# Second layer of a two-block transformer kernel: two projection chunks and eight convolution taps moved to other places in the order

## The chip, the cores and the metric

The kernel runs on one core of a Trainium2 chip. Its engines work side by side, each through its own list of instructions in the written order: TensorE (PE, matmuls; PEld is its weight load), VectorE (DVE), ScalarE (ACT), GpSimd (POOL), and SyncE (SP), which issues the DMAs. The metric is the device time of one execution in microseconds (us). Before the change the median of 3 runs is 1493.54 us (1491.67 to 1496.65).

## The reference, cut to what matters

Two blocks follow each other: a two-layer block over 256 latents `x` and 256 context rows `ctx`, and a second one over the latents alone. The change lies in the mixers of the first block's second (last) layer, where the context gives only keys and values:

```
h  = rmsnorm(x,  g_pre_mix) * (1 + sc1)  + sh1
hc = rmsnorm(xc, g_pre_mix) * (1 + sc1c) + sh1c
u  = h @ w_in
if last:
    uc_mla_kv = hc @ w_in[:, MLA_Q_END:MLA_KV_END]
    uc_na_kv  = hc @ w_in[:, NA_Q_END:]
...
kv = heads(rmsnorm(ckv, g_kv) @ w_ukv)          # the latents' norm, over 128 columns
q  = heads(rmsnorm(cq, g_q) @ w_uq)
y_mla = softmax attention over latents and context
y_cf  = silu(layernorm(dwconv(a * sigmoid(g), w_dw) + b_dw)) @ w_pw      # 31 taps
nq, nk, nv = split(u[..., CF_END:], 3)
y_na  = neighbourhood attention of nq over nk, nv and the context's nk, nv
y = concatenate([y_sc, y_mla, y_cf, y_na]) @ w_out
```

## The kernel before, in words

**Products.** Every big product is exact to about fp32: an operand is split into a high part `H` (ACT copies it, rounded) and a low part `L` (the rest, subtracted on DVE or POOL), and `mm3` (L428) issues three matmuls, H by H, L by H and H by L. `step` (L336) splits one unit of weights, 128 by 1024, so: one ACT row at L373, one DVE or POOL row at L375. Units come in the order of `weight_plan`; `pump(n)` splits them until unit n is split, `unit(name, lead)` takes the next one after having `lead` more split behind it (default 4). There are 6 buffers for split units.

**The stage.** `block1_mixers` of the second layer works on activations transposed, channels on partitions and tokens along the row: columns 0 to 255 the latents, 256 to 511 the context. A `flat_chunk` is one unit by all tokens, 24 matmuls into one PSUM bank; 256 columns wide for a chunk of the latents alone (`cq`, `nq`, `sc_*`), 512 for `nk`, which the context needs too. There are 8 banks. The order before is:

1. `token_block`: the latents' keys and values by token (`tok` of tiles 0 and 1), then `latent_chunks` (`cq0`, `cq1`), then `ctx_part`: the context's normed rows are transposed on PE (`hT`), scaled (`hF`) and split into `hH` and `hL` on ACT and DVE, eight of each; then `latent_scales` (`cqss`, and a small rsqrt chain on ACT and DVE); then `pump` splits `nq0` and `nq1`; then `tok` of tiles 2 and 3, the context.
2. The rows of `tok` are copied out, their squares summed, and `normed` makes `ckvn`, the normed latents, from them: a short chain ACT, DVE, ACT.
3. `nq0`; `kv_transposed` (PE turns `ckvn` and `kr4`, ACT copies out `ckvT`); `nq1`; `latent_heads` (`kn`, `q`, `vm`).
4. `attention`: 11 slots. Slot i computes the scores `S` of item i (0 to 3 MLA, 4 to 7 neighbourhood), turns the probabilities of item i-2 (`PT`) and multiplies those of item i-3 by the values (`PV`). Each softmax is a chain: DVE takes the maximum, ACT the exponential, DVE the reciprocal, DVE and ACT the scaling. Between them stand fillers, put into the slots by their costs: `nk0`, `nk1`, six chunks of a short convolution (`sc_*`), and the first products of `w_out` (`o`). The conformer branch ends among the slots in a layer norm (`lnT`, `lnB`) and the pointwise product `pw`, put at slots 5, 7 and 9 (`CF_SLOTS`).

**Taps.** The conformer's convolution has 31 taps for each of two channel halves: half 0 on DVE (L1019), half 1 as an ACT row (L1025) and a POOL row (L1026). They stand in two queues, and `background(n0, n1)` issues the next n0 and n1 of them wherever it is called: after `tok` (2 for each tile, half 0 alone), in each `flat_chunk` (4 and 4 in this layer unless told otherwise) and in each slot (1 and 1). What is left when `lnT` comes is issued there.

The scheduler is off (`manual_schedule`), so each engine's order is the order of the Python calls.

Of the kernel before, what the change touches and what calls it, by code (L numbers as in the profile page):

```python
# [42 lines left out]
MODS = 8, 2, 2, 2, 2, 2, 2  # L43
# [14 lines left out]
TOK_TAPS = 3, 2  # L58
# [18 lines left out]
def _r(a, n):  # L77
    return np.arange(a, a + n)
# [17 lines left out]
def weight_plan():  # L96

    p = []

    def u(name, fn):  # L100
        p.append(("u", name, fn))

    left = []

    def mods(n):
        for _ in range(n):
            if left:
                l, v, k = left.pop(0)
                p.append(("u", ("mod", l, v, k), lambda w, l=l, v=v, k=k:
                          w["w_mod"][l][128 * k:128 * k + 128, 1024 * v:1024 * v + 1024]))  # L110

    def chunk(key, l, c0, name):
        u(name, lambda w, l=l, c0=c0: _stationary(w[key][l], _r(c0, 128)))

    left += [(0, v, q) for v in (0, 2, 4, 3, 5) for q in range(8)]
    left += [(1, v, q) for v in (1, 0, 2, 4, 3, 5) for q in range(8)]
    for l in range(2):
        n_in = 1 if l == 0 else 0
        if l == 0:
            for k in range(0, 8, 4):  # L120
                for nm, c0 in (("a", 1184), ("g", 1440)):
                    u(f"{nm}_{k}", lambda w, c0=c0, k=k: _stationary(w["w_in"][0][128 * k:128 * k + 512], _r(c0, 256)))
            mods(8)
        else:
            for m in range(2):
                chunk("w_in", l, 1184 + 128 * m, f"a{m}")
                chunk("w_in", l, 1440 + 128 * m, f"g{m}")
        for j in range(4):
            u(f"tok{j}", lambda w, l=l, j=j: _moving(w["w_in"][l], (2 * j, 2 * j + 1), TOK_COLS))
        mods(MODS[0] * n_in)  # L130
        for nm, c0 in (("cq", 768), ("nq", 1696), ("nk", 1952)):
            for m in range(2):
                chunk("w_in", l, c0 + 128 * m, f"{nm}{m}")
                mods(n_in * MODS[{"cq": 1, "nq": 3, "nk": 5}[nm] + m])
        for m in range(2):
            for j, (i, nm) in enumerate(((2, "sc_c"), (0, "sc_x"), (1, "sc_b"))):
                chunk("w_in", l, 256 * i + 128 * m, f"{nm}{m}")
                mods(n_in * SC_MODS[3 * m + j])
        for h in range(2):
            for j, kk in enumerate(OUT_ORDER):  # L140
                u(f"out{h}", lambda w, l=l, kk=kk, h=h: _moving(w["w_out"][l], kk, _r(512 * h, 512)))
                mods(n_in * OUT_MODS[4 * h + j])
        if l == 0:
            for g in range(9):
                if g < 8:
                    for j in range(4):
                        chunk("w_mlp1", l, 512 * g + 128 * j, "m1")
                        mods(M1_MODS[g][j])
                if g > 0:
                    for j in range(4):  # L150
                        u("m2", lambda w, l=l, c=4 * (g - 1) + j: _moving(w["w_mlp2"][l], (c,), _r(0, 1024)))
                    mods(sum(M2_MODS[g]))
            mods(100)
        else:
            def down(c):
                u("m2", lambda w, l=l, c=c: _moving(w["w_mlp2"][l], (c,), _r(0, 1024)))

            for b in range(2):
                for j in range(4):
                    u(f"m1_{b}", lambda w, l=l, j=j, b=b: _moving(w["w_mlp1"][l], (2 * j, 2 * j + 1), _r(512 * b, 512)))  # L160
            for j, ds in zip(range(8, 32), MLP_DOWN):
                chunk("w_mlp1", l, 128 * j, "m1")
                for c in ds:
                    down(c)
            for c in range(26, 32):
                down(c)
    for nm in B2_BLOCKS:
        for j in range(4):
            u(nm, lambda w, j=j, c=B2_COL[nm]: _moving(w["w_in_2"][0], (2 * j, 2 * j + 1), _r(c, 512)))
    for m in range(16):  # L170
        chunk("w_in_2", 0, 6144 + 128 * m, "gate")
    for mm in range(4):
        for key in ("w_a_out_2", "w_b_out_2"):
            u(key, lambda w, key=key, mm=mm: np.concatenate(
                [_stationary(w[key][0], _r(256 * mm + 128 * i, 128)) for i in range(2)], 1))
    for h in range(2):
        for j in range(4):
            u(f"mix{h}", lambda w, j=j, h=h: _moving(w["w_mix_out_2"][0], (2 * j, 2 * j + 1), _r(512 * h, 512)))
    for b in range(2):
        for j in range(4):  # L180
            u(f"up_{b}", lambda w, j=j, b=b: _moving(w["w_up_2"][0], (2 * j, 2 * j + 1), _r(2816 * b, 512)))

    def down2(c):
        u("down", lambda w: _moving(w["w_down_2"][0], (c,), _r(0, 1024)))

    for j, ds in zip(range(4, 22), FFN_DOWN):
        chunk("w_up_2", 0, 128 * j, "up_g")
        chunk("w_up_2", 0, 2816 + 128 * j, "up_v")
        for c in ds:
            down2(c)  # L190
    for c in range(16, 22):
        down2(c)
    return p
# [110 lines left out]
class Program:  # L304
# [952 lines left out]
            y[k] = (self.k2("yH", dt=F32R), self.k2("yL", dt=F32R))  # L1257
        return y[k]

    def token_block(self, l, h, T):  # L1260

        nc, v = self.nc, self.nc.vector
        self.pool_l = False
# [7 lines left out]
        for ts in TOK_SETS[l]:  # L1271
            if ts[0] == CTX_AT and self.ctx_part:
                if self.narrow:
                    self.latent_chunks(l, h, T)
                self.ctx_part()
                self.ctx_part = None
                if self.narrow:
                    self.latent_scales(l, T)
                    self.pump(self.used + 1)
            banks = [self.ps("tok") for _ in ts]  # L1280
            for j in range(4):
                for i in range(2):
# [7 lines left out]
            for t in ts:  # L1290
# [5 lines left out]
                ps = banks.pop(0)  # L1296
# [5 lines left out]
                ps = None  # L1302
# [6 lines left out]
                                    m[:, :, None, 32:].to_broadcast([128, 2, 4, 32]), op=ALU.add)  # L1309
                elif t == 3:  # L1310
                    v.tensor_copy(kr[:, 2:4], u2[:, :, None, 128:160].to_broadcast([128, 2, 4, 32]))
            self.background(TOK_TAPS[l] * len(ts))

        def normed():
            r = self.rsqrt(ss, 4)
# [5 lines left out]
        us = a = b = u = u2 = None  # L1321
        if self.narrow:
            normed()
        else:
            self.latent_chunks(l, h, T, normed)

# [316 lines left out]
    def block1_mixers(self, l, h):  # L1643


        nc, v = self.nc, self.nc.vector
        full = l == 0
        T = 512 if full else 256
        nt = T // 128
        ranges = [(0, T)]  # L1650
        y = {}
        self.narrow = not full
        self.conformer_in(l, h, ranges, T)
        self.mla_w = ([self.k2("wuq") for _ in range(2)], self.k2("wukv"), [self.k2("cst") for _ in range(2)])
        s = self.ap["small"][l]
        for m in range(2):
            nc.sync.dma_start(self.mla_w[0][m], s[:, 512 * m:512 * m + 512])
        nc.sync.dma_start(self.mla_w[1], s[:, 1024:1536])
        for m in range(2):
            nc.sync.dma_start(self.mla_w[2][m], self.ap["c1"][:, 512 * m:512 * m + 512])  # L1660
        self.token_block(l, h, T)
        self.NQ, self.NK = [], []

        def nqk(dst, nm, n):
            ps = self.flat_chunk(nm, h, [(0, n)])
            q = self.k2(nm)
            nc.scalar.activation(q[:, :n], ps[:, :n], AF.Copy, scale=0.125 if dst is self.NQ else 1.0)
            dst.append(q)

        sc = self.short_conv(l, 0, h, ranges, T, y) + self.short_conv(l, 1, h, ranges, T, y)  # L1670
        nqk(self.NQ, "nq0", T)
        if full:
            self.latent_scales(l, T)
        self.kv_transposed(l)
        nqk(self.NQ, "nq1", T)
        self.latent_heads(l, T)
        self.mla_w = None
        sets = 2 if full else 1
        m = 4 * sets
        cost = 2.56 * sets  # L1680
        fl = [(lambda m=m: nqk(self.NK, f"nk{m}", 512), 5.1, 0, "") for m in range(2)]
        fl += [(f, cost, 0, "sc") for f in sc]
        banks = []

        def first(j):
            return [(f, 2.56, (0, CF_SLOTS[l][2] + 1, m + AHEAD + 1, 0)[j], "sc", 1) for f in self.out_parts("out", OUT_ORDER, y, nt, j, banks)]

        def gates():
            self.ga = self.gate_rows(l, 0, nt // 2)

        cf = self.conformer_out(l, T, y)
        fl += first(0) + first(1) + [(gates, 0.0, 0, "")]
        if full:
            fl += first(2)
        self.attention(l, sets, y, fl, dict(zip(CF_SLOTS[l], cf)))
        self.NQ = self.NK = self.VN = None
        if full:
            for f in first(3):
                f[0]()
        self.y, self.banks = y, banks  # L1700
# [823 lines left out]
```

## Time and profile before

| | |
|---|---|
| median of 3 runs | 1493.54 us |
| the profiled execution, its own time | 1495.41 us |
| its span | 1493.2 us |
| PE busy | 1428.6 us (96%) |
| PEld busy | 1194.3 us (80%) |
| DVE busy | 941.1 us (63%) |
| ACT busy | 768.4 us (51%) |
| POOL busy | 544.0 us (36%) |
| shares of the chain that ended last | PE 72%, DVE 16%, ACT 8%, issue 2%, DMA 1% |

Busy time is a share of the whole span; a busy PE is not PE at its peak, since matmuls overlap and their ends are modelled, so that a matmul's cost in a row of equal ones is the distance between two starts. The stage of the change lies between 664 and 816 us. In a row of the timeline the first number is the start in us from the span's start, the second the duration; in brackets stands how long the engine was idle ahead of it and what released it.

### The profile page before, as it was taken

The numbers are of one execution on the slowest core, as the hardware profiler recorded it, in microseconds if no ns is written. First come the engines' busy times: TensorE is split into PE (matmuls) and PEld (weight loads), VectorE is DVE, ScalarE is ACT, GpSimd is POOL, SyncE is SP. The second block draws the span as 40 slices with busy tenths as digits, with TensorE's granted clock in tenths as the row PEclk, the third lists the DMA queues.
The fourth block names the chain that finished last, engine by engine and source line by source line (L and its number), as shares of the span: only waits on it lengthen the run. The fifth ranks groups of instructions, "written<-read, shape, count | busy, mean of one in ns | idle before, by whom it ended". The sixth has DMA issues, their size and how long they took to land.

```text
span 1493.2 us, 21581 instructions
## 1 busy us (share of the span) xinstructions
PE 1428.6 (96%) x8260; PEld 1194.3 (80%) x8260; DVE 941.1 (63%) x1642; ACT 768.4 (51%) x1406; POOL 544.0 (36%) x351
## 2 busy tenths in 40 slices
PE   8989999999999998998899899998999999999998
PEld 7766767888778787877777689996888899789997
DVE  4685573765866676788776765556466666754335
ACT  4446564555553323345666554455434664556554
POOL 2384531203551500007263500005022555738882
PEclk9999999999999999998999999999999999999999
DMA  9653631124554553634242455555555433545551
GB/s 342 211 199 142 140 110 69 60 83 165 178 194 160 191 204 130 220 146 149 87 84 93 142 187 180 187 180 189 180 188 190 138 122 113 203 148 186 177 190 57
DMA packets 73103, 235.71 MB, mean 158 GB/s; under 512 B 13536, under 2 KB 14248, under 8 KB 73000
## 3 DMA queue, kind: packets, MB, share of 16 engines
q1 hardware_dynamic: 72280, 233.65, 46.3%
q8 instruction: 65, 1.06, 0.3%
q10 hardware_dynamic: 720, 0.69, 0.1%
q14 instruction: 38, 0.31, 0.1%
HBM read 233.27 MB, written 1.05 MB: 157 GB/s over the span
## 4 chain that ended last, share of the span: by engine, by line
PE 72%; DVE 16%; ACT 8%; issue 2%; DMA 1%; SPq 0%; DVEq 0%; ACTq 0%
PE m L431 8%; PE m L432 8%; PE m L430 8%; PE acc L430 3%; PE acc L431 3%; PE acc L432 3%; DVE L L375 3%; PE pj L431 2%; PE pj L430 2%; PE pj L432 2%; PE up L430 2%; PE up L432 2%; PE up L431 2%; ACT H L373 2%; ACT P L1447 1%
## 5 line engine op out<-in xcount | busy, mean ns | idle before, releaser
L375 POOL TENSOR_TENSOR L<-raw,H 128x1024 fp32r<-128x1024 f32 x117 | 283.3, 2443 | 323.0 <-ACT H L373 305.6
L373 ACT ACTIVATE H<-raw 128x1024 fp32r<-128x1024 f32 x314 | 317.3, 1050 | 131.4 <-PE m L432 48.1
L375 DVE TENSOR_TENSOR L<-raw,H 128x1024 fp32r<-128x1024 f32 x197 | 254.6, 1321 | 90.4 <-ACT H L373 87.8
L367 POOL TENSOR_TENSOR uL<-raw,uH 128x512 fp32r<-128x512 f32 x32 | 46.1, 1472 | 192.1 <-ACT uH L366 192.1
L431 PE MATMUL m<-hL,H 128*128 128x512 f32 (+1 forms) x304 | 109.0, 358 | 2.0 <-DVE hL L875 2.0
L430 PE MATMUL m<-hH,H 128*128 128x512 f32 (+1 forms) x304 | 109.0, 358 | 1.0 <-ACT hH L874 1.0
L432 PE MATMUL m<-hH,L 128*128 128x512 f32 (+1 forms) x304 | 108.7, 358 | 1.2 <-DVE L L375 1.2
L431 PE MATMUL m<-L,hidH 128*128 128x512 f32 x256 | 101.7, 397 | 4.2 <-DVE L L375 4.2
L1807 ACT ACTIVATE rl<-m 128x512 f32<-128x512 f32 (+1 forms) x56 | 28.3, 505 | 150.3 <-PE m L432 150.1
L430 PE MATMUL m<-H,hidH 128*128 128x512 f32 x256 | 101.7, 397 | 3.9 <-DVE hidL L1815 3.9
L432 PE MATMUL m<-H,hidL 128*128 128x512 f32 x256 | 100.7, 393 | 0.0
L690 POOL TENSOR_TENSOR macc<-mt,macc 128x512 f32<-128x512 f32 x42 | 61.1, 1494 | 92.3 <-ACT mt L688 92.3
L1026 POOL TENSOR_TENSOR cfacc<-cft,cfacc 128x512 f32<-128x512 f32 (+1 forms) x60 | 64.6, 1077 | 54.7 <-ACT cft L1025 50.8
L430 PE MATMUL up<-h,H 128*128 128x256 f32 x288 | 81.8, 284 | 0.0
L432 PE MATMUL up<-h,L 128*128 128x256 f32 x288 | 81.5, 283 | 0.0
L431 PE MATMUL up<-h,H 128*128 128x256 f32 x288 | 81.5, 283 | 0.0
L1814 DVE TENSOR_TENSOR m<-m,rl 128x512 f32<-128x512 f32 (+1 forms) x56 | 32.7, 584 | 76.6 <-ACT rl L1807 76.4
L696 DVE SCALAR_TENSOR_TENSOR macc<-raw,csil,macc 128x512 f32<-128x512 f32 x98 | 66.9, 749 | 0.0
L431 PEld LDWEIGHTS m<-hL,H 128*128 128x128 f32 x304 | 57.7, 190 | 10.9 <-DVE hL L875 2.6
L432 PEld LDWEIGHTS m<-hH,L 128*128 128x128 f32 x304 | 57.8, 190 | 10.1 <-DVE L L375 2.0
L430 PEld LDWEIGHTS m<-hH,H 128*128 128x128 f32 x304 | 57.9, 190 | 9.2 <-ACT hH L874 1.2
L2099 POOL TENSOR_TENSOR ra<-ra,rb 128x512 f32<-128x512 f32 x16 | 21.6, 1351 | 113.8 <-DVE rb L2097 113.3
(547 smaller groups left out, 4060.5 us busy)
## 6 DMA issues: line engine op xcount, KB each, us to landing
raw<-in_wst SPq DMA_DIRECT2D x208, 1024.0 KB
mod<-in_wmod SPq DMA_DIRECT2D x16, 256.0 KB
X<-in_x SPq DMA_DIRECT2D x4, 512.0 KB
nab<-in_rpb SPq DMA_DIRECT2D x32, 64.0 KB
raw<-in_wst SPq DMA_DIRECT2D x2, 512.0 KB
wuq<-in_small SPq DMA_DIRECT2D x4, 256.0 KB
cst<-in_c SPq DMA_DIRECT2D x4, 256.0 KB
grow<-in_rows SPq DMA_DIRECT2D x4, 256.0 KB
```

Source lines behind the costliest of these rows:

```text
L367: nc.gpsimd.tensor_tensor(lo, src, hi, op=ALU.subtract)
L373: nc.scalar.activation(hi, t[:, j, :], AF.Copy)
L375: (nc.gpsimd if pool else nc.vector).tensor_tensor(lo, t[:, j, :], hi, op=ALU.subtract)
L430: mm(out, a[0], b[0], start=start, stop=False)
L431: mm(out, a[0], b[1], start=False, stop=False)
L432: mm(out, a[1], b[0], start=False, stop=stop)
L690: nc.gpsimd.tensor_tensor(o, t, o, op=ALU.add)
L696: v.scalar_tensor_tensor(acc[i][j], a, c, o, op0=ALU.mult, op1=ALU.add)
L1026: nc.gpsimd.tensor_tensor(acc, t, acc, op=ALU.add)
L1807: nc.scalar.activation(r[:, :T], ps[:, :T], AF.Relu)
L1814: v.tensor_tensor(ps[:, :T], ps[:, :T], r[:, :T], op=ALU.mult)
L2099: self.nc.gpsimd.tensor_tensor(a, a, b, op=ALU.add)
```

## The change

In the second layer alone (`self.narrow`): `nq0` is issued inside `token_block`, behind `latent_scales` and ahead of `tok` of the context, where `pump` stood, with one unit split ahead and no taps; `nk0` is issued where `nq0` stood, ahead of `kv_transposed`, with two units split ahead and no taps, and the attention's list of fillers begins with `nk1`; the four taps of half 0 behind `tok` of the context are issued after `normed` instead of ahead of it; and the weights' order in this layer has `nk0` ahead of `nq1`. The first layer keeps its order.

```
@@ weight_plan
-        for nm, c0 in (("cq", 768), ("nq", 1696), ("nk", 1952)):
-            for m in range(2):
-                chunk("w_in", l, c0 + 128 * m, f"{nm}{m}")
-                mods(n_in * MODS[{"cq": 1, "nq": 3, "nk": 5}[nm] + m])
+        for nm, m in (("cq", 0), ("cq", 1), ("nq", 0), *((("nq", 1), ("nk", 0)) if l == 0 else (("nk", 0), ("nq", 1))),
+                      ("nk", 1)):
+            chunk("w_in", l, {"cq": 768, "nq": 1696, "nk": 1952}[nm] + 128 * m, f"{nm}{m}")
+            mods(n_in * MODS[{"cq": 1, "nq": 3, "nk": 5}[nm] + m])
@@ token_block
-    def token_block(self, l, h, T):
+    def token_block(self, l, h, T, nq):
...
                 if self.narrow:
                     self.latent_scales(l, T)
-                    self.pump(self.used + 1)
+                    nq()
...
-            self.background(TOK_TAPS[l] * len(ts))
+            if not self.narrow or ts[-1] < 3:
+                self.background(TOK_TAPS[l] * len(ts))
...
         if self.narrow:
             normed()
+            self.background(2 * TOK_TAPS[l])
@@ block1_mixers
-        self.token_block(l, h, T)
         self.NQ, self.NK = [], []
 
-        def nqk(dst, nm, n):
-            ps = self.flat_chunk(nm, h, [(0, n)])
+        def nqk(dst, nm, n, lead=None, taps=None):
+            ps = self.flat_chunk(nm, h, [(0, n)], lead, taps)
...
+        self.token_block(l, h, T, lambda: nqk(self.NQ, "nq0", T, 1, (0, 0)))
         sc = self.short_conv(l, 0, h, ranges, T, y) + self.short_conv(l, 1, h, ranges, T, y)
-        nqk(self.NQ, "nq0", T)
         if full:
+            nqk(self.NQ, "nq0", T)
             self.latent_scales(l, T)
+        else:
+            nqk(self.NK, "nk0", 512, 2, (0, 0))
         self.kv_transposed(l)
...
-        fl = [(lambda m=m: nqk(self.NK, f"nk{m}", 512), 5.1, 0, "") for m in range(2)]
+        fl = [(lambda m=m: nqk(self.NK, f"nk{m}", 512), 5.1, 0, "") for m in range(len(self.NK), 2)]
```

In the program's rows a name ends in the numbers of its buffer; `H_1318` and `L_1318` are `nq0`'s weights, `H_1319` is the second of the pair. On PE, behind the context's transposes, before:

```order
L1365 MATMUL cqss_1311_6546<-ones_150,cqs_1297_6490 128x1
L430 MATMUL tok_1321_6577<-H_1233_6133,hH_1200_6031 128x448
L431 MATMUL tok_1321_6577<-L_1233_6134,hH_1200_6031 128x448
L432 MATMUL tok_1321_6577<-H_1233_6133,hL_1201_6032 128x448
```

And the same place in the changed program:

```order
L1368 MATMUL cqss_1311_6546<-ones_150,cqs_1297_6490 128x1
L430 MATMUL nq0_1321_6577<-hH_1200_6031,H_1318_6567 128x256
L431 MATMUL nq0_1321_6577<-hL_1201_6032,H_1318_6567 128x256
L432 MATMUL nq0_1321_6577<-hH_1200_6031,L_1318_6568 128x256
```

The 24 rows of `nq0` now stand between `cqss` and the 48 rows of `tok`; its first row reads `H_1318`, its third `L_1318`.

On ACT the end of the context's split, `latent_scales` and what follows, before:

```order
L868 ACTIVATE hF_1310_6540<-hT_1306_6519,modT_1_0_4825,modT_1_1_4442 128x256
L874 ACTIVATE hH_1212_6043<-hF_1309_6536 128x256
L874 ACTIVATE hH_1214_6045<-hF_1310_6540 128x256
L450 ACTIVATE rs_y2_1314_6554<-cqss_1312_6551,eps_151 128x2
L451 ACTIVATE rs_y2_1314_6554<-rs_y2_1314_6554 128x2
L373 ACTIVATE H_1318_6567<-raw_1226_6097 128x1024
L373 ACTIVATE H_1319_6571<-raw_1226_6097 128x1024
L1298 ACTIVATE VN_1323_6627<-tok_1321_6577 128x256
```

And in the changed program:

```order
L868 ACTIVATE hF_1310_6540<-hT_1306_6519,modT_1_0_4825,modT_1_1_4442 128x256
L874 ACTIVATE hH_1212_6043<-hF_1309_6536 128x256
L874 ACTIVATE hH_1214_6045<-hF_1310_6540 128x256
L450 ACTIVATE rs_y2_1314_6554<-cqss_1312_6551,eps_151 128x2
L451 ACTIVATE rs_y2_1314_6554<-rs_y2_1314_6554 128x2
L373 ACTIVATE H_1318_6567<-raw_1226_6097 128x1024
L373 ACTIVATE H_1319_6571<-raw_1226_6097 128x1024
L1669 ACTIVATE nq0_1322_6602<-nq0_1321_6577 128x256
L373 ACTIVATE H_1325_6654<-raw_1235_6141 128x1024
L1299 ACTIVATE VN_1326_6658<-tok_1323_6604 128x256
```

`H_1318` stands at the same place on ACT in both programs, behind the context's last `hH` and the two rows of `latent_scales`; behind it the changed program has `nq0`'s copy and one more split, `H_1325`, which is `nq1`'s.

On DVE the rows about the latents' norm (`rs_*4`, which leads to `ckvn`) and up to the first `QT`, before:

```order
L1311 COPY kr4_1287_6393<-kv_1324_6628 128x256
L1019 SCALAR_TENSOR_TENSOR cfacc_1289_6398<-cfz_1_0_6210,cfw1_651,cfacc_1289_6398 128x256 x4
L452 TENSOR_SCALAR rs_x4_1327_6642<-kvss_1266_6320,eps_151 128x4
L458 TENSOR_TENSOR rs_z4_1329_6644<-rs_y4_1328_6643 128x4
L459 TENSOR_TENSOR rs_z4_1329_6644<-rs_z4_1329_6644,rs_x4_1327_6642 128x4
L460 TENSOR_SCALAR rs_z4_1329_6644<-rs_z4_1329_6644 128x4
L463 TENSOR_TENSOR rs_y4_1328_6643<-rs_y4_1328_6643,rs_z4_1329_6644 128x4
L375 TENSOR_TENSOR L_1331_6658<-raw_1235_6141,H_1331_6657 128x1024
L375 TENSOR_TENSOR L_1332_6662<-raw_1235_6141,H_1332_6661 128x1024
L375 TENSOR_TENSOR L_1334_6668<-raw_1248_6247,H_1334_6667 128x1024
L1019 SCALAR_TENSOR_TENSOR cfacc_1289_6398<-cfz_1_0_6210,cfw1_651,cfacc_1289_6398 128x256 x4
L1340 COPY KTe_1344_6726<-krT_1342_6715 64x512
```

And in the changed program:

```order
L1312 COPY kr4_1287_6393<-kv_1327_6659 128x256
L452 TENSOR_SCALAR rs_x4_1330_6669<-kvss_1266_6320,eps_151 128x4
L458 TENSOR_TENSOR rs_z4_1332_6671<-rs_y4_1331_6670 128x4
L459 TENSOR_TENSOR rs_z4_1332_6671<-rs_z4_1332_6671,rs_x4_1330_6669 128x4
L460 TENSOR_SCALAR rs_z4_1332_6671<-rs_z4_1332_6671 128x4
L463 TENSOR_TENSOR rs_y4_1331_6670<-rs_y4_1331_6670,rs_z4_1332_6671 128x4
L1019 SCALAR_TENSOR_TENSOR cfacc_1289_6398<-cfz_1_0_6210,cfw1_651,cfacc_1289_6398 128x256 x4
L375 TENSOR_TENSOR L_1334_6689<-raw_1235_6141,H_1334_6688 128x1024
L1343 COPY KTe_1341_6733<-krT_1339_6722 64x512
```

Four taps moved behind the norm's chain, and the four that `nq0` issued before are gone from here; they stand in the attention's slot 2, where the changed program has five taps of half 0 and the one before one; slots 0, 1 and 3 have 5, 5 and 4 in both.

## Rows read from the trace of the kernel before

**Rows 1.** Timeline of PE, 710 to 728 us, cqss to nq0

```profile
710.33 1.10 PE L1365 MATMUL cqss<-ones,cqs 128*128 128x1 f32 x8
712.81 0.47 PE L430 MATMUL tok<-H,hH 128*128 128x448 f32 x1 [1.38 <-ACT hH L874]
...
720.05 0.37 PE L430 MATMUL tok<-H,hH 128*128 128x448 f32 x1
...
724.39 0.28 PE L430 MATMUL nq<-hH,H 128*128 128x256 f32 x1
...
727.14 0.28 PE L432 MATMUL nq<-hH,L 128*128 128x256 f32 x1
```

**Rows 2.** Timeline of ACT, then of DVE, 717 to 722 us

```profile
717.76 0.30 ACT L450 ACTIVATE rs_y<-cqss,eps 128x2 f32<-128x2 f32 x1 [0.59 <-DVE cqss L1368]
...
718.20 1.99 ACT L373 ACTIVATE H<-raw 128x1024 fp32r<-128x1024 f32 x2
...
719.28 2.36 DVE L375 TENSOR_TENSOR L<-raw,H 128x1024 fp32r<-128x1024 f32 x2
```

**Rows 3.** Windows: busy us of PE, PEld, DVE, ACT, POOL, granted clock, DMA

```profile
86.00:88.00 2.00, 0.27 (x2) 0.12 (x2) 1.98 (x3) 0.00 (x0) 2.00 (x2) 1.00 0.73 281
...
712.00:714.00 2.00, 1.19 (x5) 0.97 (x6) 1.52 (x4) 1.47 (x4) 0.00 (x0) 0.91 0.00 0
714.00:716.00 2.00, 2.00 (x7) 1.80 (x6) 1.70 (x6) 1.81 (x6) 0.00 (x0) 0.50 0.00 0
716.00:718.00 2.00, 2.00 (x9) 1.81 (x9) 1.80 (x6) 1.22 (x4) 0.00 (x0) 0.74 0.00 0
```

**Rows 4.** Timeline of PE, 677 to 683 us, a chunk at half clock

```profile
677.47 0.58 PE L431 MATMUL ag<-hL,H 128*128 128x256 f32 x1 [1.52 <-DVE hL L875]
...
680.41 0.41 PE L432 MATMUL ag<-hH,L 128*128 128x256 f32 x1
...
682.54 0.41 PE L430 MATMUL a<-hH,H 128*128 128x256 f32 x1
```

**Rows 5.** Timeline of PE, 728 to 752 us, ckvT to nk0

```profile
728.59 1.21 PE L1331 MATMUL ckvT<-ident,ckvn 128*128 128x128 f32 x4 [1.17 <-ACT ckvn L1318]
...
734.75 1.55 PE L1381 MATMUL kn<-ckvT,wukv 128*128 128x512 f32 x3 [1.65 <-ACT ckvT L1335]
...
741.45 2.22 PE L1397 MATMUL vm<-wukv,ckvT 128*128 128x256 f32 x8 [1.26 <-ACT nq L1667]
743.50 1.88 PE L1435 MATMUL S<-KTe,QT 128*128 128x512 f32 x4
...
745.91 0.40 PE L430 MATMUL nk<-hH,H 128*128 128x512 f32 x1
...
750.02 0.39 PE L430 MATMUL nk<-hH,H 128*128 128x512 f32 x1
```

**Rows 6.** Timeline of DVE, then of ACT, 725 to 734 us, norm and taps

```profile
725.19 2.06 DVE L1019 SCALAR_TENSOR_TENSOR cfacc<-cfz,cfw,cfacc 128x256 f32<-128x256 f32 x4
...
728.13 1.28 ACT L1318 ACTIVATE ckvn<-kv,rs_y 128x128 f32<-128x128 f32 x4 [1.84 <-DVE rs_y L463]
729.32 2.94 ACT L373 ACTIVATE H<-raw 128x1024 fp32r<-128x1024 f32 x3
732.17 1.69 ACT L1025 ACTIVATE cft<-cfz,cfw 128x256 f32<-128x256 f32 x4
```

**Rows 7.** Waits of DVE, then of PE, first S to pw: us, times, longest

```profile
DVE rd L1449 <- ACT P L1447: 12.1, 8, 2.3
...
DVE sccv L1624 <- ACT sccv L1623: 1.2, 2, 0.6
...
DVE mx L1438 <- PE S L1435: 0.6, 2, 0.5
...
PE S L1464 <- ACT P L1447: 1.3, 1, 1.3
```

**Rows 8.** The window of the attention, first S to pw; columns as in Rows 3

```profile
743.50:808.64 65.14, 61.77 (x389) 46.63 (x388) 46.82 (x96) 44.87 (x92) 33.90 (x26) 1.00 0.40 96
```

## The prediction

> **What bounds the kernel now.** I read the table first: PE is busy 96% of the span and holds 72% of the last chain, so a microsecond of PE idleness removed or added in a stage that PE sets goes straight to the end. Then the timeline of PE through the stage. Ahead of the attention PE waits four times, each for a result that another engine has just made: 1.38 us for the context's `hH` [rows 1], 1.17 us for `ckvn`, 1.65 us for `ckvT`, and 1.26 us for a bank that ACT must empty [rows 5]. Between the first and the second of these PE also runs part of `tok` at half clock: the granted clock is 0.91 from 712 to 714 us, 0.50 to 716 and 0.74 to 718, about 3.4 us in all [rows 3].
>
> Inside the attention it looks different. From the first `S` to `pw` PE is busy 61.77 of 65.14 us, DVE 46.82, ACT 44.87 [rows 8]. But the waits say who leads: DVE waits there for ACT 12.1 us ahead of the reciprocals, and for PE only 0.6 us, both times at the very start; PE waits for ACT's exponentials [rows 7]. DVE and ACT hand work to each other in one unbroken chain (maximum, exponential, reciprocal, scaling, taps, next maximum), and PE's fillers, `nk0` among them, lie beside it. So two stages with different limits meet at the first `S`.
>
> **The change part by part.** 1. *`nq0` ahead of the context's `tok`.* It is there to fill PE's 1.38 us wait. It can't start then: its weights are split on ACT and DVE at the places where they were split before. ACT reaches the pair of `H` at 718.20 us, behind the context's eight `hH` and the rsqrt of `latent_scales`; a pair takes 1.99 us, so `H_1318` is there at 719.2. DVE reaches the `L` pair at 719.28 and needs 2.36 us for two, so `L_1318` is there at 720.46 [rows 2]. PE's last `cqss` row ends at 711.43 [rows 1]. PE works in order, and the 48 rows of `tok`, which before went on at 712.81, are now queued behind `nq0`; nobody can pass it. The wait grows from 1.38 to 7.8 us, and `nq0`'s third row waits for `L_1318` until 720.46. From there 22 rows of 0.12 us (727.14 less 724.39 is 2.75 for 23 rows) take 2.6 us, and 48 rows of `tok` of 0.207 us (21 rows from 720.05 to 724.39) take 9.9: both are issued at 733.0 us. Before, both were issued at 727.26, one row behind 727.14. That is **+5.8 us**, half-clock matmuls of before included on that side.
>
> 2. *The clock behind that wait.* Before, 3.4 us at half clock came after the 1.38 us wait and the broken stretch ahead of it [rows 3]; a wait of 1.7 us at 86 us was not followed by any [rows 3]. [...] After a wait of 7.8 us the clock will have fallen; how much of the low stretch lies in the wait itself the rows don't say. The bounds: nothing, if the clock is back by 720.5; 2.4 us, if the low stretch is as long as the one from 677.47 to 682.74, 5.3 us [rows 4], all 22 rows of `nq0` at 0.213 and some of `tok`. I take the 3.4 us that this very place shows, sixteen rows by 0.093: **+1.5 us**.
>
> [...]
>
> 3. *`nk0` ahead of `kv_transposed`.* 24 rows of 0.228 us (18 rows from 745.91 to 750.02) are 5.5 us [rows 5]. They cover the wait for `ckvn`: that chain needed 5.0 us from `nq0`'s first row at 724.39 [rows 1], right behind `tok`, to the end of `ckvn` at 729.41, four taps of 2.06 us on DVE among it [rows 6], and these taps now stand behind it. They also cover `ckvT`: ACT's list now has `nk0`'s copy and `ckvT`'s ahead of three splits (2.94 us) and four taps (1.69 us), not behind them [rows 6], while PE has `nq1`. And the bank that `vm` waited for is `nq1`'s; its copy stands behind those splits and taps, some 7 us after `ckvT`, while PE has `nq1`, `kn` and `q` to do, about 9. So all three waits go: **-4.1 us** (1.17, 1.65 and 1.26). What then comes latest ahead of `S` is DVE's `QT`, behind three splits and four taps, by my count a microsecond early; I cost it at nothing, and at 1 us if that cover is gone. The rows of `nk0` themselves now stand ahead of the first `S`: **+5.5 us**.
>
> 4. *What the attention gives back.* It has one filler less on PE, 5.5 us. If PE set the pace it would give them all back. But DVE waits for PE only 0.6 us there [rows 7], so the chain of DVE and ACT doesn't see `nk0` at all. The chain gets longer: the four taps that `nq0` issued before stand in slot 2 now, 2.06 us by [rows 6], while the short convolution's rows move one slot forward and one 0.6 us wait for `sccv` is covered by taps [rows 7]. **+1.4 us**, bounds -0.6 (POOL's and DVE's rows fall better) and +3. POOL's four adds move with the taps; it is busy 33.9 of 65 us [rows 8]. The DMA list of SP is the same in both programs.
>
> The sum: 5.8 + 1.5 - 4.1 + 5.5 + 1.4 = **+10.1 us**, with PE idle some 9 us in the attention instead of 3.4. Behind `pw` both programs have the same rows on PE without a wait, so the whole delay reaches the end. The profiled execution has a span of 1493.2 us and took 1495.41, 2.2 us beside the span; the sum makes it 1503.3 and 1505.5. It stands 1.9 us above the median shown, 1493.54; from that, **1503.6 us**.
>
> **The rivals.** *PE sets the pace in the attention.* For it speaks that PE is busy 61.77 of 65.14 us [rows 8]; then `nk0`'s 5.5 us come back and the taps cost nothing there: 10.1 - 5.5 - 1.4 = +3.2 us, 1496.7; if PE's 3.4 idle us are filled too, -0.2, 1493.3: not slower by more than a measurement tells. Against it: the 12.1 us that DVE waits for ACT, and the 0.6 for PE [rows 7].
>
> [...] The waits decide for me, +10.1.
>
> *`nq0`'s weights are ready at 711 us.* Then 2.9 us of `nq0` fill the gap, the context's rows are all there when `tok` starts, and both are issued at 711.4 + 2.9 + 9.9 = 724.2, 3.1 us earlier than before; with -4.1 for the waits and `nk0` given back by the attention the sum is -7.2 us, 1486.3: faster. The point from which it decides is whether `H_1318` gets onto ACT ahead of 712 us; for it speaks that ACT is idle just ahead of the rsqrt [rows 2]; against it, that the order of ACT's list is the same as before at that place.
>
> *The attention's chain stretches further.* With five taps in each of slots 0 to 2 beside the splits, DVE is late for the first half of `y`, and PE waits for it at `o`: +3 for the chain and another 3 there, +15, 1508.
>
> **How the numbers follow.** The forecast has 0.70; PE setting the pace 0.19; the early weights 0.06; the longer chain 0.05. A difference under 0.3%, 4.5 us, can't be told from none. The forecast's own range, by the bounds of the clock (-1.5, +0.9), of `QT` (+1) and of the chain (-2, +1.6), is +6.5 to +13.5, all of it slower; the longer chain is slower too; the first rival is the same, and the second faster: faster 0.06, same 0.19, slower 0.75. The range that leaves out 2 in 10 takes in the upper half of the first rival and most of the longer chain: 1496 to 1508.
>
> **What would show it.** In the profile after: a PE wait of about 7.8 us ahead of the first `nq` row, released by ACT's L373, and a granted clock of 0.5 near it; no wait ahead of `ckvT`, `kn` and `vm`; the first `S` some 8 to 9 us later than 743.50; more idle PE in the attention than the 3.4 us of before, waiting for ACT's exponentials or DVE; `pw` some 10 us later. The prediction is wrong if PE's wait ahead of `nq0` is short, or if the first `S` is late but `pw` is not.

## The result and the profile after

The changed kernel takes 1505.05 us in the median of 6 runs (1500.06 to 1505.87), the kernel before, on the same chip, 1496.37 (1491.67 to 1497.28). The ratio is 1.0055, with 95% between 1.004 and 1.007: slower, by about 8.2 us. The forecast was 1503.6, +10.1 on the kernel before. That 1503.6 lies only 1.5 us under the measured time is partly luck: the forecast started from 1493.54, and the kernel before measured 2.8 us more here. The difference is what counts, and it was 1.9 us too high.

The profiled execution has a span of 1503.1 us against 1493.2. Of these 9.9 us, 1.65 lie ahead of the change: the last `cqss` row ends at 713.08 instead of 711.43, with the same instructions on PE up to there. So every place below is counted from the end of `cqss`; what is left is +8.25, about what the ratio says.

| Stretch | before | after | difference | forecast |
|---|---|---|---|---|
| `cqss` to the end of `tok` and `nq0` | 15.83 | 23.09 | +7.26 | +7.3 |
| from there to the first `S` | 16.24 | 16.27 | +0.03 | +1.4 |
| first `S` to `pw` | 65.14 | 66.21 | +1.07 | +1.4 |
| `pw` to the end of the span | 684.56 | 684.45 | -0.11 | 0 |

The timeline of PE after (start, duration, engine, line, what, and in brackets the idle time before it with its releaser) answers to [rows 1, 5]:

```profile
712.03 1.05 PE L1368 MATMUL cqss<-ones,cqs 128*128 128x1 f32 x8
720.92 0.58 PE L430 MATMUL nq<-hH,H 128*128 128x256 f32 x1 [7.84 <-ACT H L373]
...
722.18 0.58 PE L432 MATMUL nq<-hH,L 128*128 128x256 f32 x1 [0.46 <-DVE L L375]
...
726.44 0.37 PE L430 MATMUL tok<-H,hH 128*128 128x448 f32 x1
...
736.17 0.40 PE L430 MATMUL nk<-hH,H 128*128 128x512 f32 x1
...
741.63 0.60 PE L1334 MATMUL ckvT<-ident,ckvn 128*128 128x128 f32 x4
...
745.38 1.88 PE L1384 MATMUL kn<-ckvT,wukv 128*128 128x512 f32 x4
747.10 3.62 PE L1391 MATMUL q<-cq,wuq 128*128 128x256 f32 x16
750.55 1.89 PE L1400 MATMUL vm<-wukv,ckvT 128*128 128x256 f32 x8
752.44 1.98 PE L1438 MATMUL S<-KTe,QT 128*128 128x512 f32 x4
```

PE stands still for 7.84 us ahead of `nq0`, for 0.46 us at its third row, and waits no more until the first `S`. The pair that it waits for is split where it was split before [rows 2], behind the context's `hH` and the rsqrt; ACT, then DVE:

```profile
719.39 0.29 ACT L450 ACTIVATE rs_y<-cqss,eps 128x2 f32<-128x2 f32 x1 [0.59 <-DVE cqss L1371]
719.71 0.20 ACT L451 ACTIVATE rs_y<-rs_y 128x2 f32<-128x2 f32 x1
719.82 1.99 ACT L373 ACTIVATE H<-raw 128x1024 fp32r<-128x1024 f32 x2
```

```profile
720.89 2.36 DVE L375 TENSOR_TENSOR L<-raw,H 128x1024 fp32r<-128x1024 f32 x2
```

The windows (busy us of PE, PEld, DVE, ACT, POOL; granted clock; DMA share, GB/s), which answer to [rows 3], show a granted clock of 0.50 (the lower clock in what follows) in the wait and through most of `nq0`, and the full one, 1.00, for `tok`:

```profile
714.00:716.00 2.00, 0.00 (x0) 0.00 (x0) 1.42 (x4) 1.81 (x6) 0.00 (x0) 0.86 0.00 0
716.00:718.00 2.00, 0.00 (x0) 0.00 (x0) 1.85 (x6) 1.70 (x5) 0.00 (x0) 0.50 0.00 0
...
722.00:724.00 2.00, 1.82 (x8) 1.82 (x9) 1.25 (x2) 0.00 (x0) 0.00 (x0) 0.50 0.00 0
724.00:726.00 2.00, 2.00 (x13) 2.00 (x12) 0.00 (x0) 0.00 (x0) 0.00 (x0) 0.58 0.83 213
726.00:728.00 2.00, 2.00 (x14) 1.90 (x13) 0.00 (x0) 1.30 (x2) 0.00 (x0) 1.00 0.77 311
```

The attention, in the same columns, then its waits (us in all, times, longest), against [rows 8] and [rows 7]:

```profile
752.44:818.65 66.21, 59.28 (x365) 43.33 (x365) 47.45 (x101) 45.51 (x94) 37.58 (x30) 0.95 0.38 88
```

```profile
DVE rd L1452 <- ACT P L1450: 10.8, 8, 1.8
...
DVE mx L1441 <- PE S L1438: 0.6, 2, 0.4
...
PE S L1467 <- ACT P L1450: 4.3, 1, 4.3
```

PE has 24 matmuls less to do and is done no earlier: its idle time doubles, from 3.4 to 6.9 us, 4.3 of them in one wait for an exponential, which ends at 782.28. The granted clock falls in that wait too (1.00 from 778 to 780 us, 0.57 to 782) and is 0.50 for the rows behind it:

```profile
782.00:784.00 2.00, 1.72 (x4) 1.01 (x6) 0.94 (x3) 1.77 (x6) 0.00 (x0) 0.50 0.00 0
```

The remaining rows are busy for 59.28 us; at full clock, 1.00 granted in the mean, the same rows take 56.50 (experiment e4). So 2.8 us of what `nk0` left free went into slower rows, and that is why PE is idle for 6.9 us and not for the "some 9" of the forecast.

### The profile page after: what moved, and what is told of

The parts are those of the page before. It is cut to its first block, busy times and chain, and to the rows that moved or that the text cites. A ratio compares the mean times of both kernels' runs of the same rounds, so it can differ in the third digit from the quotient of the medians.

```text
span 1503.1 us, 21589 instructions
## 1 busy us (share of the span) xinstructions
PE 1432.5 (95%) x8260; PEld 1197.1 (80%) x8260; DVE 940.7 (63%) x1643; ACT 768.0 (51%) x1406; POOL 540.8 (36%) x350
## 4 chain that ended last, share of the span: by engine, by line
PE 74%; DVE 15%; ACT 6%; issue 2%; DMA 2%; POOL 0%; SPq 0%; DVEq 0%; ACTq 0%; POOLq 0%
PE m L431 8%; PE m L432 8%; PE m L430 7%; PE acc L431 3%; PE acc L430 3%; PE acc L432 3%; DVE L L375 3%; PE pj L431 2%; PE pj L430 2%; PE pj L432 2%; PE up L430 2%; PE up L432 2%; PE up L431 2%; ACT H L373 1%; DVE h L912 1%
## 5 line engine op out<-in xcount | busy, mean ns | idle before, releaser
L430 PE MATMUL pj<-H,h 128*128 128x512 f32 x160 | 62.8, 392 | 0.0
```

Source lines behind the costliest of these rows:

```text
L430: mm(out, a[0], b[0], start=start, stop=False)
```

## The experiments

The theory going in: the loss is `nq0`'s wait for its split; `nk0`'s move costs nothing ahead of `S`, and gives nothing back in the attention, because DVE and ACT set the pace there. The rivals: `nk0`'s 5.5 us ahead of `S` are the loss; or PE sets the attention's pace. Each run was timed in five rounds beside the kernel before. All of them in one table; "`S`" is the first `S` behind the end of `cqss`, "taps" are those of DVE and of ACT issued in the attention, "PE" is PE's busy time there, "drawn out" is explained further down:

| Run | `S` | attention | taps | PE | drawn out | ratio to before, 95% |
|---|---|---|---|---|---|---|
| before | 32.07 | 65.14 | 15, 16 | 61.77 | 6.9 | 1 |
| changed | 39.36 | 66.21 | 19, 20 | 59.28 | 5.6 | 1.0055 [1.004, 1.007] |
| e1 | 31.85 | 66.48 | 19, 20 | 59.53 | 5.6 | 1.0005 [0.9994, 1.0016] |
| e2 | 38.65 | 67.88 | 19, 20 | 63.16 | 5.4 | 1.0064 [1.0051, 1.0076] |
| e3 | 32.07 | 64.96 | 15, 16 | 59.09 | 6.7 | 0.9993 [0.9984, 1.0003] |
| e4 | 32.98 | 58.67 | 9, 12 | 56.50 | 3.6 | 0.9968 [0.9956, 0.9979] |
| e5 | 32.13 | 66.40 | 19, 20 | 59.45 | 5.9 | 1.0003 [0.9994, 1.0012] |
| e6 | 40.68 | 65.66 | 19, 20 | 58.58 | 5.8 | 1.0059 [1.0045, 1.0073] |
| e7 | 31.62 | 64.92 | 11, 16 | 62.64 | 5.7 | 1.0001 [0.999, 1.0012] |
| e8 | 33.65 | 63.42 | 9, 12 | 61.08 | 8.1 | 0.9998 [0.9988, 1.0008] |
| e9 | 32.90 | 58.69 | 9, 12 | 56.51 | 3.7 | 0.9963 [0.9951, 0.9975] |
| e10 | 35.81 | 62.71 | 3, 12 | 58.99 | 7.1 | 1.0004 [0.9994, 1.0014] |
| e11 | 32.71 | 62.39 | 9, 20 | 58.17 | 6.8 | 0.9986 [0.9977, 0.9994] |
| e12 | 37.83 | 66.81 | 19, 20 | 59.88 | 5.6 | 1.0054 [1.004, 1.0068] |

**e1: `nq0`'s weights split earlier.** In `token_block` of the changed kernel, behind `latent_chunks`:

```
                     self.latent_chunks(l, h, T)
+                    self.pump(self.used)
```

> The changed kernel with one edit: nq0's weights are split between the latents' chunks and the context's part, so ahead of the context's eight hH rows, not behind them. Theory (the 7.84 us wait of the changed kernel is the place of that split): H is there about when cqss ends, L about 1.7 us later, the wait ahead of nq0 falls from 7.84 to under 1 us and that ahead of its third row to under 2; nq0 and tok take 15 to 16.5 us from the end of cqss instead of 23.1; the first S comes 6 to 8 us earlier, the attention keeps its 66 us, and the time is 0 to +2 us against the kernel before (the changed one stood at +8.7). Rival (the wait hangs on something else, a bank or the context's rows): the wait stays over 5 us, and the time stays at +6 to +10.

The 7.84 us wait is gone:

```profile
711.66 0.36 PE L430 MATMUL nq<-hH,H 128*128 128x256 f32 x1 [0.18 <-ACT H L373]
```

0.18 us are left of it, and 0.96 ahead of the third row; the first `S` comes 7.5 us earlier, and the whole is the kernel before again: the wait is the loss. That the order the change writes down gains nothing even without the wait is the second half of the answer.

**e5: the move of `nq0` alone undone.** The `nq()` ahead of `tok` goes back to `self.pump(self.used + 1)`, and `nq0` stands behind `tok`, ahead of `nk0`.

> The changed kernel with the move of nq0 alone undone: nq0 stands behind the context's tok again (as in the kernel before), nk0 stays ahead of kv_transposed, the taps stay behind the norm. Theory (the 7.84 us wait and its half-clock rows are the loss, and nk0's move by itself costs little because its 5.5 us fill waits of about 5.3 us): no PE wait over 1.5 us ahead of tok, no wait ahead of ckvT, kn and vm, the first S 32 to 33 us behind the last cqss row (39.36 in the changed kernel, 32.07 before), the attention 66 to 67 us as in the changed kernel; against the kernel before +0.5 to +2.5 us. Rival (nk0's 5.5 us ahead of the first S are the loss): +4.5 to +7 us, the first S 36 to 38 us behind cqss.

As the theory has it: no wait ahead of `ckvT`, `kn` and `vm`, the first `S` 0.06 us later than before with 5.5 us of `nk0` ahead of it, the whole at 1.0003 of before, a little under the +0.5 to +2.5 us expected. `nk0`'s move is free.

**e2: `nk0` alone back among the fillers.** The changed kernel without its line for `nk0`, the plan's order again `nq1`, `nk0`.

> The changed kernel with nk0 back among the attention's fillers, and nothing in its place ahead of kv_transposed. Theory (the attention's pace is set by DVE and ACT, so nk0's 5.5 us on PE cost nothing there): PE waits about 4 us for ckvn, the first S is 1 to 2 us earlier than in the changed kernel, the attention from the first S to pw stays at 65 to 67 us, and the time is 0.5 to 3 us under the changed kernel's, +5.5 to +8 against the kernel before. Rival (PE sets the pace in the attention): there nk0's 5.5 us are added, the stretch is 70 us or more, and the time is 3 to 5 us above the changed kernel's, +11.5 to +14.

Both missed: the whole is about what the changed kernel takes. `nk0` covered 3 us of waiting:

```profile
739.33 1.35 PE L1334 MATMUL ckvT<-ident,ckvn 128*128 128x128 f32 x4 [3.04 <-ACT ckvn L1320]
```

so the first `S` comes only 0.7 us earlier, and the attention is 1.7 us longer with `nk0` in it, neither the same nor 5.5 us more. The 1.7 us aren't `nk0`'s price alone: PE's waits fall elsewhere in this attention. The longest, 3.19 us at 795.24, ends with the first of two `nab` rows of DVE, which beside a row of POOL took 2.49 us where it takes 0.68 alone (before, at 784.7 us):

```profile
792.64 3.09 DVE L1419 TENSOR_TENSOR nab<-nab,nam 128x512 f32<-128x512 f32 x2
```

**e3: PE alone relieved.** The kernel before with seven eighths of `nk1`'s products left out (21 of 24 matmuls, 4.8 us; its values are then another matrix's):

```
-        self.chunk(u, h, ranges, ps)
+        self.chunk(u, h, ranges, ps, range(1) if self.narrow and name == "nk1" else range(8))
```

> The kernel before with seven eighths of nk1's products left out in the second layer (3 of its 24 matmuls remain, in the attention's slot 1; its copy, its split and its taps stay). Theory: 21 rows of 0.228 us, 4.8 us, go from PE in the attention, and the stretch from the first S to pw stays at 64 to 65.5 us with 4 to 5 us more PE idle; the time is the same, -1 to +0.5 us. Rival (PE sets the pace there): the stretch is 60 to 61.5 us, the time -4 to -5.

The attention shrinks by 0.2 us; the time turns into waits of PE, and part of what is left of PE's rows runs at the lower clock (0.95 in the mean):

```profile
745.09:810.05 64.96, 59.09 (x368) 44.91 (x367) 46.66 (x96) 44.76 (x92) 33.65 (x26) 0.95 0.41 96
```

```profile
PE PT L1519 <- ACT P L1447: 2.4, 1, 2.4
PE PT L1519 <- ACT nk L1667: 2.2, 1, 2.2
```

**e7: the taps alone moved.** The kernel before, with 4 taps on DVE and 8 on ACT behind the `pump` ahead of `tok`, the last two tiles' taps behind `normed`, none on ACT beside `nq0` and `nq1`:

```
                     self.pump(self.used + 1)
+                    self.background(4, 8)
```

> The kernel before (nq0, nk0 where they were) with the taps alone moved: 4 taps on DVE and 8 on ACT into the wait for the context's splits, the taps of tok's last two tiles behind the norm, none on ACT beside nq0 and nq1. Theory (DVE's and ACT's chain sets the attention's pace, and these engines have idle time ahead of the first S): the waits for ckvn, ckvT and vm shrink to 0.5 to 2.5 us together (4.1 before), the attention takes 62 to 64 us instead of 65.1, the whole -3 to -5 us against the kernel before. Rival (PE, busy 95% of the attention, sets its pace): the attention stays at 64 to 65.5 us and only the waits ahead of the first S go, -1 to -2.5 us.

The rival's attention, and not even its 1 to 2.5 us on the whole. Four taps less on DVE shorten the attention by 0.2 us; DVE waits instead (`rd` for ACT's `P` 14.1 us, one of 4.3, where [rows 7] has 12.1 and 2.3), while PE is busy 62.64 of 64.92 us. With e3 this says that before, two limits lay nearly level in the attention, PE's own rows and the chain of DVE and ACT: taking this much from one alone gives 0.2 us, whichever it is.

**e4: both at once.** e1, with ten taps on DVE and eight on ACT issued beside the idle engines ahead of the context's `tok`:

```
                     nq()
+                    self.background(10, 8)
```

> The changed kernel with nq0's weights split early, and with ten taps of half 0 and eight of half 1 issued behind nq0, ahead of the context's tok, where DVE and ACT have nothing else to do. Theory: the attention has ten DVE taps less, 5 us of a chain that sets its pace, and nk0's 5.5 us less on PE than the kernel before, so that both limits fall; the first S stands where it does in the run with the early split alone, the stretch to pw is 60 to 62.5 us instead of 66, and the time -3 to -6 us against the kernel before. Rival (the chain's length comes from the softmaxes and their hand-overs, the taps only fill gaps): the stretch stays at 64 to 66 us, and the time at -1 to +2.

The attention takes 58.67 us, 6.5 less than before and less than the 60 to 62.5 expected, and PE is idle in 2.2 of them:

```profile
744.37:803.04 58.67, 56.50 (x365) 42.25 (x365) 40.32 (x91) 42.31 (x86) 31.55 (x22) 1.00 0.43 99
```

e1 has the same rows on PE ahead of and in the attention. Of the 7.8 us by which e4's attention is shorter than e1's, 4.8 are idle time of PE, and 3.0 are rows that no longer run at the lower clock (0.95 in the mean in e1, 1.00 here). The first `S` comes 1.1 us later than in e1, with waits of 0.48 us for `ckvn` and 0.81 ahead of `vm`. This version beats both kernels: 1490.71 us, 0.32% under before.

**e8: e4 with `nk0` back in the attention.** The edit of e2, in e4.

> The version with the early split of nq0 and ten taps on DVE and eight on ACT behind nq0 (4.8 us under the kernel before), with nk0 back among the attention's fillers. Theory (with the chain of DVE and ACT shortened to 58.7 us by the taps, PE sets the attention's pace, so nk0 costs there what it takes): the first S 1.5 to 3.5 us earlier, behind a wait for ckvT of 2 to 3.5 us, the attention 62 to 64.5 us, the whole +1 to +4 us against that version, -1 to -4 against the kernel before. Rival (the chain still sets the pace): the attention 58.5 to 60.5 us, the whole -5.5 to -7.5 against the kernel before.

The theory's attention (63.42 us), but not its first `S`, which comes 0.7 us later than in e4 where 1.5 to 3.5 us earlier was expected: the wait for `ckvn` is 4.45 us, and in this profile most of `nq0`'s rows stood 0.21 us apart, as at the lower clock, not 0.12 (+1.5). The whole is 4.5 us above e4 by the two ratios, a little more than the 1 to 4 expected, so that nothing is left against the kernel before. In the attention PE's rows are the floor: 61.08 us of them with `nk0`, and 2.3 idle. With `nk0` in it, six taps less on DVE and four less on ACT than before bring 1.7 us and no more. So `nk0`'s move pays little as long as the chain is as long as PE's list, and 4.75 of its 5.5 us in the attention once the chain is shorter (58.67 against 63.42).

**e9: e4 without `nq0`'s move.** e5 with the same ten and eight taps ahead of `tok`.

> nq0 behind the context's tok, as in the kernel before, nk0 ahead of kv_transposed as in the changed kernel, and ten taps on DVE and eight on ACT issued ahead of tok, beside the splits. Theory (what pays is the pair of nk0's move and fewer taps in the attention; nq0's move pays nothing even with its weights split early): the first S 32 to 34 us behind the last cqss row, the attention 58 to 60 us, the whole -4 to -6.5 us against the kernel before, within 1.5 us of the version with nq0 ahead (-4.8). Rival (nq0 ahead of tok is a part of that gain): -1 to -3 us, with the missing time in front of the first S.

1490.83 us, 0.37% under before, level with e4: the move of `nq0` gives nothing even when it costs nothing. The gain is `nk0` and the taps together.

**e10 and e11: how many taps, and whose.** e4 with `background(16, 8)`, and with `background(10, 0)`.

> The version 4.8 us under the kernel before, with sixteen instead of ten taps on DVE behind nq0. Theory (at 58.7 us, of which PE is busy 56.5, PE sets the attention's pace, so that six more taps taken from DVE there bring little): the attention 57.5 to 58.7 us, the first S 0 to 2 us later, the whole -3 to -5.5 us against the kernel before. Rival (DVE's chain still sets it): the attention 55 to 57 us, the whole -6 to -8.

> The version 4.8 us under the kernel before with the ten taps on DVE alone behind nq0; the eight on ACT (with POOL's adds) stay in the attention. Theory (DVE's taps make the chain longer: ten of 0.52 us; ACT's waiting rows are short): the attention 59 to 62 us, the whole -2 to -4.5 us against the kernel before. Rival (ACT's and POOL's taps are what stretches the chain): the attention 64 to 66.5 us, the whole -1 to +1.

e11 lies where the theory had it, within 0.4 us: DVE's taps bring half of the gain, ACT's and POOL's the other half. e10 missed both readings: six taps fewer in the attention, and it is 4 us longer than e4's. The first `S` is late because `ckvn` stands behind the taps (a 1.81 us wait where e4 has 0.48) and `nq0` fell to the lower clock (0.50 granted from 718 to 720 us, +1.5). Inside, one wait of 1.5 us for an exponential is followed by the lower clock (0.50 granted from 780 to 784 us, 0.95 in the mean, 58.99 us for the rows that take 56.50 in e4), and DVE, with less to do, has longer rows than e4 at the same place (the row of e10, then of e4):

```profile
770.05 3.42 DVE L1421 TENSOR_TENSOR nab<-nab,nam 128x512 f32<-128x512 f32 x2
```

```profile
765.65 1.28 DVE L1421 TENSOR_TENSOR nab<-nab,nam 128x512 f32<-128x512 f32 x2
```

**e6 and e12: the clock behind the wait.** The changed kernel with 52, then 36 matmuls of `ident` into a bank that nobody reads, ahead of `nq()`.

> The changed kernel with 52 matmuls of 128x128, whose result nobody uses, on PE right ahead of nq0, so that PE is busy for most of the 7.84 us in which it waits for H. Theory (the wait brings the half clock, and this adds 1.6 us): nq0's 22 rows take 2.6 to 2.8 us instead of 4.26, tok as before, the whole 1.5 us under the changed kernel, +6 to +7.5 us against the kernel before. Rival (the low clock at this place comes from somewhere else, such as the broken stretch ahead of the wait): the 22 rows still take 4.2 us and the time is the changed kernel's, +8 to +9.5.

> The changed kernel with 36 idle matmuls ahead of nq0 instead of 52. In the run with 52 they became 104 instructions of 0.114 us and ended at 723.03 us, some 2.6 us after L was there, so what the full clock gave was lost again. 36 (72 instructions, 8.2 us) should end about 0.8 us before L. Theory (the 7.84 us wait is what lowers the clock): the granted clock stays at 1.00, nq0's rows behind L take 2.6 to 2.8 us, nq0 and tok are issued 21.4 to 21.8 us behind the last cqss row (23.09 in the changed kernel), the whole 1.3 to 2 us under the changed kernel, +6 to +7 us against the kernel before. Rival (the attention's own clock and waits swallow it): nq0 and tok as said, but the attention 1 to 2 us longer and the whole +8 to +9.5.

Each of these matmuls is two rows on PE, 104 and 72 in all. In e6 the clock stayed at 1.00 (711 to 726 us), but the added rows ended 2.6 us behind `L` and took more than they gave: the first `S` is 1.3 us later. In e12 they ended in time:

```profile
712.92 8.30 PE L1282 MATMUL warm<-ident 128*128 128x128 f32 x72
720.98 0.36 PE L430 MATMUL nq<-hH,H 128*128 128x256 f32 x1
...
721.93 0.39 PE L432 MATMUL nq<-hH,L 128*128 128x256 f32 x1 [0.47 <-DVE L L375]
722.15 0.28 PE L430 MATMUL nq<-hH,H 128*128 128x256 f32 x1
```

```profile
720.00:722.00 2.00, 1.53 (x14) 1.33 (x13) 1.90 (x7) 1.57 (x2) 0.00 (x0) 1.00 0.00 0
722.00:724.00 2.00, 2.00 (x17) 2.00 (x18) 1.01 (x1) 0.00 (x0) 0.00 (x0) 1.00 0.00 0
```

The granted clock is 1.00 from 712 to 724 us, and `nq0` and `tok` are done 21.56 us behind `cqss` instead of 23.09: 1.5 us, the whole clock term, comes from PE standing still. On the whole time it can't be told: the attention of this profile is 0.6 us longer, and the interval holds both readings.

## Why the prediction was right, step by step

1. **`nq0`'s wait, +5.8.** Right in size and place: 7.84 us for 7.8, released by ACT's `H`, `nq0` and `tok` issued 7.26 us later (7.3 with the clock). e1 and e5 take this wait away in two ways and both give the time of before.
2. **The clock, +1.5.** Right: the 22 rows behind `L` take 4.26 us instead of 2.64, +1.6 (granted clock 0.50 from 722 to 724 us, 0.58 to 726), and `tok` runs at full clock (1.00 from 726). The 0.093 us a row of this term is 0.213, the mean of the ten distances between 680.41 and 682.54 us before (0.50 granted from 680 to 682), less 0.12. Behind this wait there were fourteen such distances, not sixteen (722.55 to 725.55, 0.214 us each), the two at their ends took 0.37 and 0.18, and the last rows stood 0.12 us apart again. e12 shows the wait as its cause.
3. **`nk0` ahead of `kv_transposed`, -4.1 and +5.5.** The mechanism held, the size of the gain was off. All three waits went, and `nk0` took 5.46 us. But the waits were worth 5.4 us, not 4.1: the row ahead of a wait runs out with nothing beside it (`nq0`'s last took 0.28 us, where the next row in its stream starts after 0.12), the rows behind it took longer than in a stream (`ckvT` and `krT` below), and I counted the idle time alone. The clock isn't the reason: 1.00 was granted from 727 to 743.5 us before the change. `ckvT` and `krT` took 1.40 us from their first row to the next chunk (728.59 to 729.99), now 0.79 (741.63 to 742.42); with `nq0`'s end (0.16), `nq1` (0.15), `kn` and `q` (0.27) and `vm` (0.16) that makes 1.35 us. This is most of the 1.9 us by which +10.1 was too high. `QT` was not late, with 0.28 us to spare (ready at 752.16, `vm` done at 752.44) where I had counted one.
4. **The attention gives nothing back, +1.4.** Right for the change: +1.07 here, and 66.4 to 66.8 us in e1, e5 and e12. The reason I gave was half of it, so the size is in part luck. I read DVE's short wait for PE as saying that PE doesn't matter; e7, e4 and e8 show that PE's list was a second limit right behind. Taking `nk0` away gains 1.7 us at most while the chain stays (e2 against the changed kernel), and 4.8 us of `nk1` gain 0.2 (e3), so the rival "PE sets the pace" failed, but the chain alone wasn't the limit either. The -0.6 and +2.06 of which I made this term weren't measured apart, and the 2.8 us of rows at the lower clock weren't in it at all.

The rival of the early weights was not what the change does; e1 builds it. The prediction gave it -7.2, with `nk0`'s 5.5 us given back by the attention; the runs give 0, and -4.8 only with the taps moved as well.

## What to carry to other kernels

Before moving an instruction into a wait, look up when its own operands are ready: PE, working in order, turned a 1.38 us gap into the operand's whole delay, 7.84 us. An engine that is busy for 95% of a stage and a chain that hardly waits for it (0.6 us here) can be two level limits, as e3, e7 and e4 showed; relieve both in one experiment before calling either free. And count a wait with the rows on both sides of it, not by its idle time alone.

## What the runs showed of the hardware

Some of DVE's short rows in the softmax chain are drawn out beside POOL. In the attention of the 14 kernels above, `P` (the scaling, 128x512 in SBUF) took 0.48 or 0.49 us in all 54 cases in which POOL was idle, and up to 2.50 us beside one of POOL's `L` rows (e8); `nb`, two numbers in each partition, took 0.16 us in the five cases in which POOL was idle and up to 2.11 beside an `L` row (before). The profile books this as busy time. In the changed kernel, DVE's rows, then POOL's, just ahead of PE's 4.3 us wait:

```profile
776.20 2.17 DVE L1419 TENSOR_TENSOR nab<-nab,nam 128x512 f32<-128x512 f32 x2
778.30 1.28 DVE L1441 TENSOR_REDUCE mx<-S 128x1 f32<-128x512 f32 x2
779.61 1.66 DVE L1442 TENSOR_TENSOR nb<-mx,nqs 128x2 f32<-128x2 f32 x1
```

```profile
774.32 4.63 POOL L1026 TENSOR_TENSOR cfacc<-cft,cfacc 128x256 f32<-128x256 f32 x5 [1.42 <-ACT cft L1025]
778.92 2.33 POOL L375 TENSOR_TENSOR L<-raw,H 128x1024 fp32r<-128x1024 f32 x1
```

`nb` is to start at 779.61 and ends at 781.27, with POOL's row (778.92 and 2.33 us). The maxima ahead of it read PSUM and are not drawn out: the pair took 1.28 us, the second of it beside the same row of POOL, and a pair of before with POOL idle 1.27 (767.19 us). The taps on DVE, which add into an accumulator in PSUM, show none of it either: all 162 that ran beside a row of POOL in these attentions took 0.47 to 0.49 us, as the others did. "Drawn out" in the table sums over the attention what each instruction of `nb`, `P` and `nab` takes beyond 0.17, 0.49 and 0.64 us, about the shortest seen: 6.9 us before, 3.6 in e4, 7.1 in e10. `nb` stands between a maximum and its exponential, so e4's gain may in part be that its rows fell well beside POOL's (its `nab` rows are not drawn out at all, those of before by 2.4 us). But e8 has the most of it, 8.1 us, with PE idle for only 2.3. No run moved POOL's rows alone, and how much of the 6.5 us that is stays open.

The clock was not the same behind the same wait: e1 and e4 both have 0.18 and 0.96 us of waiting at `nq0`, and the 22 rows behind them took 4.23 us in the profile of e1 (granted clock 0.50 from 714 to 716 us), 2.74 in that of e4 (1.00 from 712 to 718). e8, e10 and e11 have the same two waits within 0.01 us and are like e1, with 4.22 to 4.23 us. Why e4 was spared no run shows, and each is one profiled execution.
